# Hybrid decoder layer, 1 core: all tiles' normed rows turned from their buffers, operand sums from turned blocks, weight rows sooner, w_down sums in GpSimd's queue

## The chip, the core and the metric

The kernel runs on one core of a Trainium2 chip. The metric is the device time of one execution in microseconds, as a median over runs. The engines are TensorE (PE, matmuls and transposes), VectorE (DVE), ScalarE (ACT), GpSimd (POOL) and SyncE (SP). SP computes nothing here and issues most of the transfers; ACT and POOL issue a few. Each engine works through its own instructions in a fixed order.

## What is computed

One decoder layer on 2048 rows of width 1024, all in float32: a mixing part (window attention on one half of the width, a convolution group on the other), its output projection with a norm and the residual, and a gated feed-forward layer with a norm and the residual. The change touches the second half of it:

```python
hn = rms_norm(h, mix_pre_g)
proj = hn @ w_in
...
mixed = jnp.concatenate([attn_out, conv_out], axis=-1) @ w_out
h = h + rms_norm(mixed, mix_post_g)
hn = rms_norm(h, ffn_pre_g)
ff = (jax.nn.silu(hn @ w_gate) * (hn @ w_up)) @ w_down
h = h + rms_norm(ff, ffn_post_g)
```

## The kernel before

**Tiling.** The 2048 rows are four tiles `w` of 512 (`T`), each 4 × 128. A tile of an activation is held turned, 128 channels on the partitions and 512 rows along them; eight such blocks `k` (`KC`) make the width of 1024. A float32 product is made of three matmuls: each operand is split into a high part (a cast on ACT) and the rest, `lo` (a subtraction on DVE). One *product* here is four blocks `k` of three 128×512 matmuls, 12 in all.

**The feed-forward layer** runs in two passes, pass 0 over tiles 0 and 1, pass 2 over tiles 2 and 3. Each pass multiplies 2 × 2 blocks with seven products in place of eight: sums and differences of blocks (names `B11`, `B21`, `B22`, `T1` to `T4`) are multiplied and combined. Tile 0 or 2 supplies `B11` and `B21`, made by `stage_h_plain`; `stage_h_sums` makes `T1` to `T4` and `B22` from both tiles of a pass, for `k` = 0 to 3 in turn, with the tile `own` (0 or 2) and the other one.

**Phases on PE, in order:** the input projections (A), attention (B) and convolution (C), the output projection of each tile with its norm (W), then per pass `stage_pre` (40 products in pass 0, 32 in pass 2, on `B11` and then `B21`, labelled F; its partial results are stored in `keeps` and `mids`), `stage_p1` (labelled F, 22 rounds of 5 products in pass 0; it reads `keeps` and makes sums of weights on DVE) and `stage_p2` (labelled G, the second matrix). The prediction calls the `stage_p1` of pass 0 P1.0. A product whose accumulation goes on from a stored partial result starts with ACT writing that block into the PSUM bank: a *seed* (`mm@F<-gb@F`, L954 and L1066), loaded by SP from `keeps` into a buffer of the tag `gb`.

**Beside the main phase**, side jobs run in lanes: convolution taps (`fc@C`, on DVE), norms of later tiles, `stage_h_plain`, `stage_h_sums`, the end of a pass (`finish`), and `stage_tsums`, which makes the sums of `w_down` blocks (four blocks in, four sums out to `td`, eleven sets, for pass 0's G phase). Each job is a generator; its rate says how much of it is issued for each product. A scheduler then orders each engine's instructions and picks the buffers before the run. Tags have few buffers: `chl` 5, `at` 2, `gb` 2, `fc` 3, `wx` 1.

**Normed rows to turned blocks.** `norm_w` leaves the four normed row blocks of a tile in `xs` (four `chl` buffers). For tile 0 they stay there, and `stage_h_plain` turns them with `turn_row`: four PE transposes into one bank (`ct`), ACT copies it scaled into `gb`, ACT's queue stores it to `hT`. Tile 2 is turned in the norm. For tiles 1 and 3 ACT's queue stores the rows to `hn_scr` (L797); `stage_h_sums` later loads columns of them (`load_cols`, L820), and `turned` transposes these on PE (L842).

**Rounds of P1** (`stage_p1`): in step `nst - 2` a round fetches the next round's partial results, in the last step it loads the weight rows of the round after that.

Of the kernel before, what the change touches and what calls it, by code (L numbers as in the profile page):

```python
# [12 lines left out]
F32 = mybir.dt.float32  # L13
# [5 lines left out]
ALU = mybir.AluOpType  # L19
# [3 lines left out]
S = 2048  # L23
# [14 lines left out]
def layer_kernel(ctx, tc, x, xT, cols, rows, sinks, relb, onehot, w_in, w_pw, w_out, w_gate, w_up, w_down, out):  # L38
# [721 lines left out]
    def norm_w(w, acc):  # L760
        L = f"W{w}"
        lab[0] = L

        def whole(src):
            t = f4("chl")
            nc.sync.dma_start(t, src)
            return t

        gb = whole(rows[0].partition_broadcast(P))
        ssq = sm(4)  # L770
        for s in range(4):
            act(junk, acc[s], AF.Square, accum_out=ssq[:, s : s + 1])
            yield 0.75
            lab[0] = L
        r = rsqrt(ssq, 4, D, w < 3)
        xs = [whole(x[w * T + s * P : w * T + (s + 1) * P]) for s in range(4)]
        ssq2 = sm(4)
        yield 3
        for s in range(4):
            lab[0] = L  # L780
            stt(acc[s], acc[s], r[:, s : s + 1], gb, ALU.mult, ALU.mult)
            yield 1.25
            lab[0] = L
            vtt(acc[s], xs[s], acc[s], ALU.add)
            r0 = w * T + s * P
            nc.sync.dma_start(h_scr[r0 : r0 + P], acc[s])
            act(junk, acc[s], AF.Square, accum_out=ssq2[:, s : s + 1])
            yield 1.25
        lab[0] = L
        r2 = rsqrt(ssq2, 4, D, w < 3)  # L790
        yield 3
        for s in range(4):
            lab[0] = L
            act(xs[s], acc[s], AF.Copy, scale=r2[:, s : s + 1])
            if w % 2:
                r0 = w * T + s * P
                nc.scalar.dma_start(hn_scr[r0 : r0 + P], xs[s])  # L797
# [20 lines left out]
    def load_cols(w, k, tag):  # L818
        t = f2(tag, (P, 4, P))
        nc.sync.dma_start(t, hn_scr[w * T : (w + 1) * T, k * P : (k + 1) * P].rearrange("(s p) c -> p s c", p=P))  # L820
        return t

    def split_f(x, w):
        act(w[:, 0], x, AF.Copy)  # L824
# [13 lines left out]
    def turned(w, k, bank_of, tag):  # L838
        c = load_cols(w, k, tag)
        b = bank_of()  # L840
        for s in range(4):
            nc.tensor.transpose(b[:, s * P : (s + 1) * P], c[:, s], ident)  # L842
        return b
# [12 lines left out]
    def stage_h_plain(ws, ops, n, off):  # L856
        L = f"H{ws[0]}"
        for k in range(4):
            lab[0] = L
            if ws[0]:  # L860
                u = f2(COLTAG[ws[0]][k])
                nc.sync.dma_start(u, hT[ws[0] // 2][k + off])
            else:
                u = turn_row(0, normed, k + off)
                lab[0] = L
            o = op_tile(ws, ops, n, k, {})
            act(o[:, 0], u, AF.Copy)
            lo(u, o, False)
            yield 2.0

    def stage_h_sums(ws, ops):
        L = f"H{ws[0]}"
        spare = {}
        for k in range(4):
            lab[0] = L
            ct_ = COLTAG[ws[0]]
            g1, g2 = g_ffn[:, k : k + 1], g_ffn[:, k + 4 : k + 5]
# [11 lines left out]
            lab[0] = L  # L889
# [6 lines left out]
            for n, x in (("T1", r[:, 0]), ("T2", t[:, 0]), ("T3", r[:, 1]), ("T4", t[:, 1])):  # L896
# [95 lines left out]
    def stage_p1(ws, ops, mid, keep):  # L992
# [54 lines left out]
        for q, (m, j, i, nst) in enumerate(todo):  # L1047
# [60 lines left out]
            if j == nst - 1:  # L1108
                loads(m + 2)
            yield 2.76  # L1110

    def stage_tsums(td):
        L = "G0"
        for pr in range(NF // 2):
# [1 line left out]
            wx = f4("wx", (P, 2, T))  # L1116
            b = [wx[:, 0], wx[:, 1], f2("fc"), f2("fc")]
            for i, (f, n) in enumerate(((0, 0), (0, 1), (1, 0), (1, 1))):
                nc.sync.dma_start(b[i], w_down[2 * pr + f, :, n * T : (n + 1) * T])
            yield 3  # L1120
            b11, b12, b21, b22 = b
            for to, o, p_, q_ in ((0, b11, b12, b11), (2, b12, b22, b12), (1, b22, b22, b11), (3, b21, b21, b22)):
                lab[0] = L
                vtt(o, p_, q_, ALU.subtract)
                nc.sync.dma_start(td[to, pr], o)
# [412 lines left out]
```

## Time and profile before

| | us |
|---|---|
| median of 3 runs (lowest, highest) | 1996.32 (1993.41, 1996.72) |
| profiled execution | 1994.08 |
| its span | 1992.1 |
| PE busy in the span | 1936.4 |
| DVE busy | 1467.2 |
| ACT busy | 953.5 |
| POOL busy | 247.2 |

The profile is of one execution. Times in it count from the start of the span. A row of the view by stretches gives a window's start and end, its length, then for each engine the busy time and, in brackets, the instructions; PEclk is the share of TensorE's full clock that was granted, the DMA share the mean busy share of the core's 16 DMA engines. A row of the view of groups gives line, engine, operation, result <- operands, the count, then busy time and the mean of one in ns, then idle time ahead of it and what ended it. A row of the timeline gives start and duration, and in brackets the idle time before and its releaser. A row of transfers ends with the size of one and the median time from issue to landing. A name such as `gb@F` is the tag of a buffer and the phase that filled it.

### The profile page before, as it was taken

Reading aid. Unit: us, or ns where it says so; the run is one execution under the profiler, and the core shown is the slowest. Engines: PE = TensorE matmul, PEld = TensorE weight load, DVE = VectorE, ACT = ScalarE, POOL = GpSimd, SP = SyncE. Lnnn points to the kernel's source line nnn. Section 1 sums busy time; section 2 is a strip of 40 time slices with the busy share of each in tenths; the row PEclk is TensorE's granted clock in tenths of the full one; section 3 lists DMA queues with packets and bytes.
Section 4 is the critical chain, followed back from the end, with each engine's and each line's share of the span. In section 5 each row is a group of like instructions: output and inputs, shape, how many; then the busy total and the mean of one; then the engine's idle time right before and its main releaser. Section 6 shows DMA issues by size and latency. Waiting matters only on the chain.

```text
span 1992.1 us, 26622 instructions
## 1 busy us (share of the span) xinstructions
PE 1936.4 (97%) x8730; PEld 1550.4 (78%) x8730; DVE 1467.2 (74%) x2648; ACT 953.5 (48%) x1878; POOL 247.2 (12%) x339
## 2 busy tenths in 40 slices
PE   8999999999998999899999999998899999999997
PEld 6877777777776878678888788886788888888886
DVE  4999969995875899777659964667766765455557
ACT  5455354447546533234355464656543433345443
POOL 4011111101121000000000110000023332311003
PEclk9999999999999999999999999999999999999999
DMA  8786657566659767865478787759845542466664
GB/s 307 252 305 218 210 187 257 182 214 216 225 199 322 258 222 254 280 231 190 143 238 273 255 270 243 253 201 376 289 147 170 169 159 85 142 227 197 211 195 143
DMA packets 224810, 444.06 MB, mean 223 GB/s; under 512 B 22136, under 2 KB 47904, under 8 KB 224672
## 3 DMA queue, kind: packets, MB, share of 16 engines
q1 hardware_dynamic: 212768, 429.79, 64.8%
q10 hardware_dynamic: 11904, 12.59, 1.8%
q8 instruction: 68, 1.11, 0.2%
q14 instruction: 70, 0.57, 0.1%
HBM read 327.46 MB, written 114.83 MB: 222 GB/s over the span
## 4 chain that ended last, share of the span: by engine, by line
PE 77%; DMA 11%; DVE 6%; issue 2%; ACT 2%; POOL 1%; SPq 1%; DVEq 0%; POOLq 0%; ACTq 0%
PE mm@F L85 29%; PE mm@G L85 18%; PE mm@A L85 14%; PE mm@W L85 5%; PE tr@B L85 4%; PE tr@W L85 3%; DMA gb@F<-keeps 1%; DMA chl@F<-w_gate 1%; DMA raw@F<-w_gate 1%; PE mm@U L85 1%; DMA chl@G<-h_scr 1%; DVE fc@C L94 1%; DVE w@F L94 1%; DMA td<-fc@G 1%; PE tr@B L492 1%
## 5 line engine op out<-in xcount | busy, mean ns | idle before, releaser
L94 DVE SCALAR_TENSOR_TENSOR fc@C<-glu@C,colt,fc@C 128x512 f32<-128x512 f32 x480 | 357.1, 758 | 2.8
L85 PE MATMUL mm@F<-hl@H,w@F 128*128 128x512 f32 x1056 | 256.8, 394 | 8.1 <-ACT mm@F L954 8.1
L85 PEld LDWEIGHTS mm@F<-hl@H,w@F 128*128 128x128 f32 x1056 | 200.4, 190 | 51.5 <-ACT mm@F L954 9.5
L85 PE MATMUL mm@G<-hl@G,hl@G 128*128 128x512 f32 x924 | 228.0, 392 | 1.8 <-DVE hl@G L94 1.6
L85 PE MATMUL mm@A<-hl@A,w@A 128*128 128x512 f32 x840 | 209.4, 397 | 4.4 <-ACT w@A L127 1.8
L85 PEld LDWEIGHTS mm@G<-hl@G,hl@G 128*128 128x128 f32 x924 | 171.7, 188 | 38.9 <-DVE hl@G L94 2.4
L824 ACT ACTIVATE w@F<-chl@F 128x512 fp32r<-128x512 f32 x220 | 134.8, 624 | 138.9 <-PE mm@F L85 131.4
L85 PE MATMUL mm@G<-w@G,hl@G 128*128 128x512 f32 x876 | 199.4, 389 | 0.0
L85 PEld LDWEIGHTS mm@G<-w@G,hl@G 128*128 128x128 f32 x876 | 164.4, 188 | 34.1
L85 PEld LDWEIGHTS mm@A<-hl@A,w@A 128*128 128x128 f32 x840 | 156.6, 189 | 43.1 <-issue 3.1
L94 DVE TENSOR_TENSOR w@F<-chl@F,w@F 128x512 fp32r<-128x512 f32 x198 | 145.6, 739 | 37.9 <-ACT w@F L824 37.3
L85 PE MATMUL mm@F<-mid@H,w@F 128*128 128x512 f32 x528 | 137.4, 408 | 12.5 <-ACT mm@F L954 10.6
L85 PE MATMUL mm@F<-ql@H,w@F 128*128 128x512 f32 x528 | 128.5, 391 | 6.8 <-ACT mm@F L1066 4.8
L85 PE MATMUL mm@F<-p@H,w@F 128*128 128x512 f32 x528 | 132.5, 397 | 0.0
L85 PEld LDWEIGHTS mm@F<-mid@H,w@F 128*128 128x128 f32 x528 | 103.7, 198 | 36.8 <-ACT mm@F L954 11.9
L85 PE MATMUL mm@F<-x@H,w@F 128*128 128x512 f32 x528 | 126.7, 391 | 0.0
L85 PEld LDWEIGHTS mm@F<-ql@H,w@F 128*128 128x128 f32 x528 | 98.9, 188 | 29.3 <-ACT mm@F L1066 6.2
L85 PEld LDWEIGHTS mm@F<-p@H,w@F 128*128 128x128 f32 x528 | 101.7, 193 | 21.8 <-ACT at@F L1080 0.2
L85 PEld LDWEIGHTS mm@F<-x@H,w@F 128*128 128x128 f32 x528 | 98.4, 188 | 21.1 <-issue 0.8
L127 ACT ACTIVATE w@A<-raw@A 128x512 fp32r<-128x512 f32 x110 | 67.5, 626 | 92.3 <-PE mm@A L85 63.5
L94 DVE TENSOR_TENSOR w@G<-raw@G,w@G 128x512 fp32r<-128x512 f32 x73 | 52.1, 714 | 68.8 <-ACT w@G L824 67.7
L495 POOL TENSOR_SCALAR_AFFINE_SELECT p@B<-p@B 128x512 f32<-128x512 f32 x62 | 52.9, 863 | 361.2 <-ACT p@B L493 359.8
(302 smaller groups left out, 3224.8 us busy)
## 6 DMA issues: line engine op xcount, KB each, us to landing
mids<-fa@F SPq DMA_DIRECT2D x154, 256.0 KB, 2.6
raw@A<-w_in SPq DMA_DIRECT2D x55, 512.0 KB, 4.5
w@A<-lo_in SPq DMA_DIRECT2D x84, 256.0 KB, 3.5
fc@G<-mids SPq DMA_DIRECT2D x77, 256.0 KB, 3.5
fa@G<-mids SPq DMA_DIRECT2D x75, 256.0 KB, 4.2
gb@F<-keeps SPq DMA_DIRECT2D x72, 256.0 KB, 4.5
w@W<-fold SPq DMA_DIRECT2D x32, 512.0 KB, 5.3
chl@F<-w_gate SPq DMA_DIRECT2D x22, 512.0 KB, 4.0
```

The source lines that it names most:

```text
L85: r = nc.tensor.matmul(*args, **kw)
L94: r = op(*args, **kw)
L127: act(w[:, 0], raw, AF.Copy)
L492: nc.tensor.transpose(o[:, i * P : (i + 1) * P], pr[:, 4 * g + i], ident)
L495: nc.gpsimd.affine_select(out=pg[:, kb].rearrange("p (i q) -> p i q", q=P), in_=pg[:, 1].rearrange("p (i q) -> p i q", q=P), compare_op=AL ...
L824: act(w[:, 0], x, AF.Copy)
```

## The change

1. The rows of tiles 1, 2 and 3 are all turned at the end of `norm_w`, straight from `xs`, into `at` buffers. SP stores each turned block to `hT`, one turn after it was made. `hn_scr`, `load_cols` and `turned` are gone.
2. `stage_h_sums` loads two turned blocks of both tiles and forms the sums from these: four DVE operations for four, and five splits, per `k`; one cast of ACT less.
3. `stage_tsums` issues its 88 transfers from GpSimd's queue in place of SP's, and its yields and rate (`RT`) change.
4. `stage_p1` fetches partial results two steps sooner and loads weight rows two steps sooner; `y5` is in `at`, not in `gb`.
5. The sums of pass 2 (`S2`) may start after 8 steps of P2 in place of 16, but only when the job `E0.3` is done; rates of a few jobs change.

```diff
 act(xs[s], acc[s], AF.Copy, scale=r2[:, s : s + 1])
-if w % 2:
-    r0 = w * T + s * P
-    nc.scalar.dma_start(hn_scr[r0 : r0 + P], xs[s])
...
 if w == 0:
     normed.extend(xs)
-if w == 2:
-    for k in range(KC):
-        turn_row(w, xs, k)
-        yield 2.0
+    return
+late = []
+for k in range(KC):
+    late.append(turn_row(w, xs, k, "at"))
+    if k:
+        nc.sync.dma_start(hT[w // 2][w % 2, k - 1], late[k - 1])
+    yield 2.0
+nc.sync.dma_start(hT[w // 2][w % 2, KC - 1], late[-1])
...
-def turn_row(w, xs, k):
+def turn_row(w, xs, k, tag):
...
-    u = f2("gb")
+    u = f2(tag)
     act(u, b, AF.Copy, scale=g_ffn[:, k : k + 1])
-    nc.scalar.dma_start(hT[w // 2][k], u)
     return u
...
 # stage_h_sums, for k in range(4)
-own = t_("chl", (P, 2, T))
-nc.sync.dma_start(own, hT[ws[0] // 2][k :: 4].rearrange("j p t -> p j t"))
-own = own[:, 0], own[:, 1]
-b12 = turned(ws[1], k, tr, ct_[2])
-b22 = turned(ws[1], k + 4, tr, ct_[3])
+own, other = (t_("chl", (P, 2, T)) for _ in range(2))
+for j, b in enumerate((own, other)):
+    nc.sync.dma_start(b, hT[ws[0] // 2][j, k::4].rearrange("j p t -> p j t"))
+yield 2.5
+b = op_tile(ws, ops, "B22", k, spare)
+act(b[:, 0], other[:, 1], AF.Copy)
 r = t_("chl", (P, 2, T))
-t = t_("chl", (P, 2, T))
-act(r[:, 1], b12, AF.Copy, scale=g1)
-b = op_tile(ws, ops, "B22", k, spare)
-act(b[:, 0], b22, AF.Copy, scale=g2)
-yield 1.5
-stt(r[:, 0], b12, g1, own[0], ALU.mult, ALU.subtract)
-stt(t[:, 0], b22, g2, r[:, 0], ALU.mult, ALU.subtract)
-stt(r[:, 1], b22, g2, r[:, 1], ALU.mult, ALU.subtract)
-stt(b[:, 1], b22, g2, b[:, 0].bitcast(F32), ALU.mult, ALU.subtract)
-vtt(t[:, 1], own[1], t[:, 0], ALU.subtract)
-yield 3
+vtt(r[:, 0], other[:, 0], own[:, 0], ALU.subtract)
+vtt(r[:, 1], other[:, 1], r[:, 0], ALU.subtract)
+vtt(other[:, 0], other[:, 1], other[:, 0], ALU.subtract)
+lo(other[:, 1], b, False)
+vtt(own[:, 1], own[:, 1], r[:, 1], ALU.subtract)
+yield 2
...
 # stage_p1
-        y5 = f2("gb")
+        y5 = f2("at")
...
 if j == nst - 4:
+    fetch(m + 1)
     sums(m + 1)
-if j == nst - 2:
-    fetch(m + 1)
-if j == nst - 1:
+if j == nst - 3:
     loads(m + 2)
...
 # stage_tsums
-        nc.sync.dma_start(b[i], w_down[2 * pr + f, :, n * T : (n + 1) * T])
-    yield 3
+        nc.gpsimd.dma_start(b[i], w_down[2 * pr + f, :, n * T : (n + 1) * T])
+    yield 2.5
...
-        nc.sync.dma_start(td[to, pr], o)
-        yield 1
+        nc.gpsimd.dma_start(td[to, pr], o)
+        yield 0.6
...
-RT = 0.3
+RT = 0.2
...
-PRE_S0, PRE_S2 = 22, 16
+PRE_S0, PRE_S2 = 22, 8
...
-lh.rates = {"N1": 1.2, "S0": 0.9, "H0": 1.2}
-lf.rates = {n: 0.6 for n in ("O0.1", "O0.3", "E0.1", "E0.3")} | {n: 1.2 for n in ("Y0", "Y1", "O2.1", "O2.3")}
+lh.rates = {"N1": 1.2, "S0": 0.9, "B21.2": 1.2, "S2": 0.7}
+lf.rates = {n: 1.2 for n in ("O0.1", "O0.3", "E0.1", "E0.3")} | {n: 1.2 for n in ("Y0", "Y1", "O2.1", "O2.3")}
...
-lh.add("S2", stage_h_sums(ws, ops), lambda: f"P2.{PRE_S2}" in started)
+lh.add("S2", stage_h_sums(ws, ops), lambda: f"P2.{PRE_S2}" in started and "E0.3" in lf.done)
```

**PE in pass 0's `stage_pre`.** Each row is line, operation, result <- operands, shape, and a count where the next ones are alike; the numbers in a name tell one buffer's use from another. Before, the first transposes of loaded columns (`tr@H`) stand together after the 25th of the 40 products:

```order
L85 MATMUL mm@F_1010_6114<-hl@H_813_4982,w@F_992_6038 128x512 x3
L85 MATMUL mm@F_1010_6114<-hl@H_821_5029,w@F_992_6038 128x512 x3
L842 MATMUL tr@H_1002_6087<-ident,fc@H_1001_6085 128x128 x4
L842 MATMUL tr@H_1004_6094<-ident,at@H_1003_6092 128x128 x4
L842 MATMUL tr@H_1025_6191<-ident,fc@H_1024_6189 128x128 x4
L842 MATMUL tr@H_1027_6198<-ident,at@H_1026_6196 128x128 x4
L85 MATMUL mm@F_1015_6141<-hl@H_802_4928,w@F_995_6059 128x512 x3
L85 MATMUL mm@F_1015_6141<-hl@H_810_4971,w@F_995_6059 128x512 x3
```

In the changed kernel the transposes read the row buffers of the norm (`chl@W`) and write the bank `ct`. The last of the eight turns stands here, inside the 35th product (`mm@F_1085`):

```order
L85 MATMUL mm@F_1085_6455<-hl@H_802_4927,w@F_1071_6393 128x512 x3
L814 MATMUL ct@H_996_6040<-ident,chl@W_938_5731 128x128
L814 MATMUL ct@H_996_6040<-ident,chl@W_939_5733 128x128
L814 MATMUL ct@H_996_6040<-ident,chl@W_940_5735 128x128
L814 MATMUL ct@H_996_6040<-ident,chl@W_941_5737 128x128
L85 MATMUL mm@F_1085_6455<-hl@H_810_4970,w@F_1071_6393 128x512 x3
L85 MATMUL mm@F_1085_6455<-hl@H_813_4981,w@F_1071_6393 128x512 x3
```

The eight groups moved from before the middle of the stage's second half, some of them together, to one group in every two products up to its last fifth.

**DVE at the end of pass 0's `stage_pre`.** Before, the sums (`chl@H`) and splits of operands (`mid@H`, `p@H`, `hl@H`, `mb@H`) stand among the splits of weights (`w@F`):

```order
L94 TENSOR_TENSOR p@H_1065_6370<-chl@H_1052_6309,p@H_1065_6370 128x512
L94 SCALAR_TENSOR_TENSOR chl@H_1075_6413<-tr@H_1072_6401,colt,chl@H_1070_6397 128x512
L94 TENSOR_TENSOR w@F_1078_6423<-raw@F_1059_6343,w@F_1078_6423 128x512
L94 TENSOR_TENSOR mid@H_1066_6373<-chl@H_1053_6310,mid@H_1066_6373 128x512
L94 SCALAR_TENSOR_TENSOR chl@H_1076_6414<-tr@H_1074_6408,colt,chl@H_1075_6413 128x512
L94 SCALAR_TENSOR_TENSOR chl@H_1075_6413<-tr@H_1074_6408,colt,chl@H_1075_6413 128x512
L94 SCALAR_TENSOR_TENSOR hl@H_1077_6416<-tr@H_1074_6408,colt,hl@H_1077_6416 128x512
L94 TENSOR_TENSOR w@F_1083_6447<-raw@F_1079_6426,w@F_1083_6447 128x512
L94 TENSOR_TENSOR mb@H_1086_6468<-chl@H_1075_6413,mb@H_1086_6468 128x512
```

Now the last split of a weight of the stage (`w@F_1100`) comes first and the first operation of `stage_h_sums` stands right behind it:

```order
L94 TENSOR_TENSOR fa@F_1080_6440<-fa@F_1080_6440,mm@F_1079_6426 128x512
L94 TENSOR_TENSOR w@F_1100_6533<-raw@F_1090_6483,w@F_1100_6533 128x512
L94 TENSOR_TENSOR chl@H_1022_6169<-chl@H_1017_6143,chl@H_1016_6142 128x512
L94 TENSOR_TENSOR chl@H_1022_6169<-chl@H_1017_6143,chl@H_1022_6169 128x512
L94 TENSOR_TENSOR chl@H_1017_6143<-chl@H_1017_6143 128x512
L94 TENSOR_TENSOR hl@H_1021_6167<-chl@H_1017_6143,hl@H_1021_6167 128x512
L94 TENSOR_TENSOR chl@H_1016_6142<-chl@H_1016_6142,chl@H_1022_6169 128x512
L94 TENSOR_TENSOR mid@H_1023_6175<-chl@H_1022_6169,mid@H_1023_6175 128x512
L94 TENSOR_TENSOR fa@F_1093_6502<-fa@F_1093_6502,mm@F_1092_6488 128x512
L94 TENSOR_SCALAR fc@C_1099_6530<-glu@C_1098_6528,colt 128x512
```

From the first `chl@H_1022` row to the split of the first weight of P1.0, this piece's second last row, stand 57 instructions, with convolution taps (`fc@C`), `w_down` sums (`fc@G`, `wx@G`) and results of `stage_pre` (`fa@F`) among 35 of the 36 of `stage_h_sums`:

```order
L94 TENSOR_TENSOR ql@H_1087_6474<-chl@H_1082_6444,ql@H_1087_6474 128x512
L94 TENSOR_TENSOR chl@F_1110_6613<-chl@F_1110_6613,raw@F_1108_6609 128x512
L94 TENSOR_TENSOR p@H_1088_6477<-chl@H_1075_6415,p@H_1088_6477 128x512
L94 TENSOR_TENSOR fc@G_1126_6672<-fc@G_1126_6672,fc@G_1127_6673 128x512
L94 TENSOR_TENSOR w@F_1112_6619<-chl@F_1110_6613,w@F_1112_6619 128x512
L94 TENSOR_TENSOR chl@F_1111_6616<-raw@F_1108_6609,chl@F_1109_6611 128x512
```

All 36 stood before the stage's last weight split and now stand behind it.

**The queues of SP and POOL in P1.0.** Before, SP issues the `w_down` loads and `td` stores between weight rows (`chl@F`) and seeds (`gb@F`):

```order
L1125 DMA td<-fc@G_1372_8309 128x512
L1119 DMA wx@G_1403_8516<-w_down 128x512 x2
L1119 DMA fc@G_1404_8517<-w_down 128x512
L1008 DMA chl@F_1355_8184<-w_gate 128x1024
L1119 DMA fc@G_1405_8518<-w_down 128x512
L1094 DMA mids_4716<-fa@F_1310_7903 128x512
L1038 DMA gb@F_1351_8163<-keeps_4719 128x512
L1125 DMA td<-wx@G_1403_8516 128x512 x2
```

The same set of blocks (`wx@G_1403` there, `wx@G_1405` here) stands on POOL with no other work around it:

```order
L1102 DMA fc@G_1377_8333<-w_down 128x512
L1108 DMA td<-wx@G_1375_8331 128x512
L1108 DMA td<-fc@G_1377_8333 128x512
L1102 DMA wx@G_1405_8523<-w_down 128x512 x2
L1108 DMA td<-fc@G_1376_8332 128x512
L1102 DMA fc@G_1406_8524<-w_down 128x512
L1102 DMA fc@G_1407_8525<-w_down 128x512
L1108 DMA td<-wx@G_1405_8523 128x512 x2
```

**PE in pass 2's `stage_pre`.** The last turns of tile 3 stand among the first blocks (`mid@H_2045`) of four products; the next matmul needs the second block, `mid@H_2047`:

```order
L85 MATMUL mm@F_2142_12802<-mid@H_2045_12331,w@F_2129_12740 128x512 x3
L814 MATMUL ct@H_1976_11904<-ident,chl@W_1921_11605 128x128
L814 MATMUL ct@H_1976_11904<-ident,chl@W_1922_11607 128x128
L814 MATMUL ct@H_1976_11904<-ident,chl@W_1923_11609 128x128
L814 MATMUL ct@H_1976_11904<-ident,chl@W_1924_11611 128x128
L814 MATMUL ct@H_1978_11918<-ident,chl@W_1921_11605 128x128
L814 MATMUL ct@H_1978_11918<-ident,chl@W_1922_11607 128x128
L814 MATMUL ct@H_1978_11918<-ident,chl@W_1923_11609 128x128
L814 MATMUL ct@H_1978_11918<-ident,chl@W_1924_11611 128x128
L85 MATMUL mm@F_2123_12713<-mid@H_2047_12336,w@F_2109_12651 128x512
```

Before, transposes of loaded columns stood in this stage one or two groups at a time; now these last four groups have three matmuls between the first three and none between the last two.

More of the change, by code (lines that the diff above doesn't have):

```diff
@@ L241, in layer_kernel @@
     glu_scr = dr.tile([4, P, S], F32, name="glu_scr")
-    hn_scr = dr.tile([S, D], F32, name="hn_scr")
     y_scr = dr.tile([4, P, S], F32, name="y_scr")
-    hT = [dr.tile([KC, P, T], F32, name=f"hT{i}") for i in range(2)]
+    hT = [dr.tile([2, KC, P, T], F32, name=f"hT{i}") for i in range(2)]
     qs = {}
@@ L800, in norm_w @@
             normed.extend(xs)
-        if w == 2:
-            for k in range(KC):
-                turn_row(w, xs, k)
-                yield 2.0
+            return
[3 more added lines that the diff above has]
+            if k:
+                lab[0] = f"H{w}"
+                nc.sync.dma_start(hT[w // 2][w % 2, k - 1], late[k - 1])
+            yield 2.0
+        lab[0] = f"H{w}"
+        nc.sync.dma_start(hT[w // 2][w % 2, KC - 1], late[-1])
     normed = []
-    def turn_row(w, xs, k):
+    def turn_row(w, xs, k, tag):
         lab[0] = f"H{w}"
@@ L836, in layer_kernel @@
     COLTAG = {0: ["fc", "at", "fc", "at"], 2: ["fc", "at", "fc", "at"]}
[L838 to L843, printed above, removed]
     def op_tile(ws, ops, n, k, spare):
@@ L861, in stage_h_plain @@
                 u = f2(COLTAG[ws[0]][k])
-                nc.sync.dma_start(u, hT[ws[0] // 2][k + off])
+                nc.sync.dma_start(u, hT[ws[0] // 2][0, k + off])
             else:
-                u = turn_row(0, normed, k + off)
+                u = turn_row(0, normed, k + off, "gb")
                 lab[0] = L
+                nc.scalar.dma_start(hT[0][0, k + off], u)
             o = op_tile(ws, ops, n, k, {})
@@ L875, in stage_h_sums @@
             lab[0] = L
-            ct_ = COLTAG[ws[0]]
-            g1, g2 = g_ffn[:, k : k + 1], g_ffn[:, k + 4 : k + 5]
-            own = t_("chl", (P, 2, T))
-            nc.sync.dma_start(own, hT[ws[0] // 2][k :: 4].rearrange("j p t -> p j t"))
-            own = own[:, 0], own[:, 1]
-            b12 = turned(ws[1], k, tr, ct_[2])
-            b22 = turned(ws[1], k + 4, tr, ct_[3])
-            r = t_("chl", (P, 2, T))
-            t = t_("chl", (P, 2, T))
-            act(r[:, 1], b12, AF.Copy, scale=g1)
-            b = op_tile(ws, ops, "B22", k, spare)
-            act(b[:, 0], b22, AF.Copy, scale=g2)
-            yield 1.5
-            lab[0] = L
-            stt(r[:, 0], b12, g1, own[0], ALU.mult, ALU.subtract)
-            stt(t[:, 0], b22, g2, r[:, 0], ALU.mult, ALU.subtract)
-            stt(r[:, 1], b22, g2, r[:, 1], ALU.mult, ALU.subtract)
-            stt(b[:, 1], b22, g2, b[:, 0].bitcast(F32), ALU.mult, ALU.subtract)
-            vtt(t[:, 1], own[1], t[:, 0], ALU.subtract)
-            yield 3
-            for n, x in (("T1", r[:, 0]), ("T2", t[:, 0]), ("T3", r[:, 1]), ("T4", t[:, 1])):
+            own, other = (t_("chl", (P, 2, T)) for _ in range(2))
+            for j, b in enumerate((own, other)):
+                nc.sync.dma_start(b, hT[ws[0] // 2][j, k::4].rearrange("j p t -> p j t"))
+            yield 2.5
+            lab[0] = L
+            b = op_tile(ws, ops, "B22", k, spare)
+            act(b[:, 0], other[:, 1], AF.Copy)
+            r = t_("chl", (P, 2, T))
+            vtt(r[:, 0], other[:, 0], own[:, 0], ALU.subtract)
[4 more added lines that the diff above has]
+            yield 2
+            for n, x in (("T1", r[:, 0]), ("T2", r[:, 1]), ("T3", other[:, 0]), ("T4", own[:, 1])):
                 lab[0] = L
```

4 lines of the change are left out of this document (removed).

## The prediction

> **What bounds the kernel now.** I read the page first, then busy time by stretches for the stages the change touches, then who waited for whom inside them. TensorE (PE) is busy 97% of the span, so a change matters where it adds or removes PE idling; the question is where the idle time lies.
>
> ```profile
> span 1992.1 us, 26622 instructions
> PE 1936.4 (97%) x8730; PEld 1550.4 (78%) x8730; DVE 1467.2 (74%) x2648; ACT 953.5 (48%) x1878; POOL 247.2 (12%) x339
> ...
> 1003.64 2.20 PE L85 MATMUL mm@F<-ql@H,w@F 128*128 128x512 f32 x9
> 1005.68 4.70 PE L85 MATMUL mm@F<-hl@H,w@F 128*128 128x512 f32 x20
> ...
> core 0: us, PE busy (x) PEld busy (x) DVE busy (x) ACT busy (x) POOL busy (x), PEclk, DMA share, GB/s
> 610.71:682.21 71.50, 62.62 (x273) 50.48 (x272) 50.78 (x81) 46.26 (x82) 0.00 (x0) 0.95 0.89 301
> 1327.33:1438.02 110.69, 98.22 (x418) 79.31 (x416) 88.11 (x187) 74.76 (x145) 0.52 (x1) 0.94 0.96 338
> ...
> 682.21:780.00 97.79, 95.60 (x412) 77.94 (x411) 88.28 (x144) 35.72 (x64) 0.00 (x0) 0.98 0.68 225
> 780.00:900.00 120.00, 108.52 (x447) 87.11 (x446) 94.81 (x153) 39.38 (x71) 0.00 (x0) 0.94 0.78 263
> 900.00:1013.80 113.80, 113.80 (x505) 94.26 (x504) 80.68 (x126) 46.98 (x83) 0.00 (x0) 1.00 0.52 168
> ```
>
> Nine matmuls from 1003.64 to 1005.68 are 0.227 us each without a stall, so a product of 12 is 2.72 us. With that pace each stage's loss follows, idle time and slow clock together. The last 20 products of pass 0's `stage_pre` begin at 610.71; 240 matmuls are 54.4 us and the 32 transposes 4.9 (below), so of 71.5 us 12.2 are lost. The first FFN phase of pass 0 (P1.0, 682.21 to 1013.8, 331.6 us) holds 1364 PE records, 309.2 us: 22.4 lost, all before 900, for from there PE is busy throughout. Pass 2's `stage_pre` (384 matmuls, 87.1, and 4.9) loses 18.7 of 110.7. These 53 us are what the change can win or spend.
>
> **What causes the losses.** In pass 0 the normed rows of tile 1 leave in one burst on ACT's queue, and a weight load comes late behind it:
>
> ```profile
> 609.48 0.34 ACTq L797 DMA_DIRECT2D hn_scr<-chl@W  x1
> ...
> hn_scr<-chl@W ACTq DMA_DIRECT2D x4, 512.0 KB, 8.5
> ...
> 622.39 0.63 ACT L824 ACTIVATE w@F<-raw@F 128x512 fp32r<-128x512 f32 x1 [3.52 <-DMA raw@F<-w_gate]
> ...
> 624.05 1.22 PE L85 MATMUL mm@F<-hl@H,w@F 128*128 128x512 f32 x2 [3.71 <-ACT mm@F L954]
> ```
>
> The seed that PE waited for stands behind the weight cast on ACT. In P1.0 the late one is another seed, behind the `w_down` loads and `td` stores in SP's queue:
>
> ```profile
> 863.49 1.93 SPq L1119 DMA_DIRECT2D wx@G<-w_down  x2
> 865.51 0.38 SPq L1119 DMA_DIRECT2D fc@G<-w_down  x1
> ...
> 867.37 0.42 SPq L1038 DMA_DIRECT2D gb@F<-keeps  x1
> ...
> 874.13 0.60 ACT L1066 ACTIVATE mm@F<-gb@F 128x512 f32<-128x512 f32 x1 [6.59 <-DMA gb@F<-keeps]
> ...
> SPq L1125 <- DVE wx@G L94: 21.2, 15, 4.3
> SPq L1119 <- DMA td<-fc@G: 21.0, 9, 4.7
> SPq L1119 <- DMA td<-wx@G: 15.8, 8, 4.2
> ...
> SPq L1125 <- DVE fc@G L94: 10.7, 17, 1.6
> ...
> PE mm@F L85 <- DVE gb@F L94: 5.0, 3, 2.2
> PE mm@F L85 <- ACT mm@F L1066: 4.8, 2, 4.5
> ```
>
> SP stood 68.7 us in these four waits, with seeds and weight rows queued behind.
>
> **The change, part by part: pass 0's turns.** Instruction counts on PE and DVE do not change; their places do. Eight turns of four transposes stand two products apart, the last three matmuls into the 35th of 40 products. The old transposes price them, their busy time being a little over what they occupy:
>
> ```profile
> L842 PE MATMUL tr@H<-ident,at@H 128*128 128x128 f32 x16 | 2.5, 276 | 0.7 <-DVE chl@H L94 0.7
> L842 PE MATMUL tr@H<-ident,fc@H 128*128 128x128 f32 x16 | 2.4, 272 | 0.0
> ...
> chl@H<-hT SPq DMA_DIRECT2D x3, 512.0 KB, 4.8
> ...
> 700.00:750.00 50.00, 48.78 (x206) 39.84 (x207) 46.54 (x76) 18.62 (x34) 0.00 (x0) 0.97 0.66 216
> ...
> 610.71 1.52 PE L85 MATMUL mm@F<-hl@H,w@F 128*128 128x512 f32 x6
> ...
> 682.21 1.52 PE L85 MATMUL mm@F<-ql@H,w@F 128*128 128x512 f32 x6
> ```
>
> From 610.71, 14 products (38.1), three matmuls (0.7) and 32 transposes (4.9) put the last turn's end at 654.4, with 1 us for a stall that stays at 655.4. Until then the four rows hold four of the five `chl` buffers, and the first `other` block of `stage_h_sums` can be loaded only after: 4.8 us. What VectorE (DVE) then has before P1.0's first product is the point. Before, the sums stood among the weight splits; now all stand behind the last split, mixed with conv taps and `w_down` sums, 57 instructions in order to the split of P1.0's first weight. A DVE that rarely waits does 76 in 46.54 us, 0.612 each: 34.9 us, and 1 us for waits on ACT's casts. P1.0 starts at 655.4 + 4.8 + 34.9 + 1 = 696.1 instead of 682.21: **+13.9**, the relief of the burst already counted. PE has ended its own products near 671 and idles some 25 us. Bounds: no stall in the stage and DVE at its pace alone, +10; the 12.2 us lost as before with 4 us more for load and casts, +24.
>
> **The clock.** Stretches with long stalls show a lower granted clock:
>
> ```profile
> 1360.00:1420.00 60.00, 47.53 (x194) 37.35 (x193) 47.48 (x98) 37.18 (x70) 0.00 (x0) 0.89 1.01 350
> ```
>
> 47.53 busy us at 0.89 are 5.2 us lost to the clock around several stalls; an idle of 25 us costs part of it, **+2** (0 to 4).
>
> **P1.0.** SP loses 88 issues and the four waits, to GpSimd's queue, where nothing else stands (POOL x0 above). Seeds and rows are asked for two products sooner, 5.4 us; the worst seed was 6.59 late. Counting DVE instructions to each weight split against PE's products, the splits run 3 to 16 us ahead after some ten products; at the start the second weight's split comes about 2 us after PE wants it. I keep 9 of the 22.4 lost: 2 there, 7 for seeds still late and `w_down` blocks that DVE waits for. **−13.4**; bounds −22.4 and +4 (queue slower, as in the rival). DVE keeps its 88.28 of 97.79 us, so it has no reserve for such waits early on. This trace has no transfer in GpSimd's queue. By the nearest rows a block lands in about 4 us and so does a store:
>
> ```profile
> wx@G<-w_down SPq DMA_DIRECT2D x20, 256.0 KB, 4.0
> td<-fc@G SPq DMA_DIRECT2D x22, 256.0 KB, 3.5
> ```
>
> Ten sets of four blocks pass between 682 and 900, 22 us each; a set takes at least 4.0 + four sums (2.4) + 3.5 = 10 us, since the one `wx` buffer is not free sooner. The spare 12 us hide a slower queue, and I cost it at nothing. The Trainium skill, "SBUF — State Buffer", section "SBUF: two separate sides", warns against this very move: while DVE runs a two-port instruction GpSimd cannot write descriptors, and it gives 620 ns growing to 3100 ns beside a copy. By its "Who interferes with whom" a two-input `tensor_tensor` has no such mode, and the groups of DVE here are nearly all of that kind, so by the skill the sum stays; no run here yet shows it.
>
> **Pass 2.** Four turns of tile 3 stand apart, then four in one clump in the 17th round of products, three matmuls between, because `at` has two buffers and each is freed by a store. The second block of B21 needs one of them.
>
> ```profile
> PE mm@F L85 <- ACT mm@F L954: 10.6, 4, 4.1
> ...
> raw@F<-w_gate SPq DMA_DIRECT2D x12, 256.0 KB, 6.1
> ...
> at@H<-hn_scr SPq DMA_DIRECT2D x4, 256.0 KB, 6.8
> ...
> 1327.33 2.88 PE L85 MATMUL mm@F<-ql@H,w@F 128*128 128x512 f32 x12
> ...
> 1438.02 2.20 PE L85 MATMUL mm@F<-hl@H,w@F 128*128 128x512 f32 x9
> ```
>
> The clump ends near 1327.3 + 16 × 2.72 + 4.9 + 1.4 = 1377. A store and then a load in this crowded stretch take some 6 us each, cast and split 1.3: PE idles to 1391, about 14 us, 2 more at the fourth block, 2 for the clock, 2 for loads as late as now: 20 against 18.7 lost, **+1**. Bounds −8 (a store that went before lets the load start at once) and +7. `y5` in `at` and the spread of the `w_down` sums (the same work in 270 as in 257 units of the plan) lie under PE time: nothing; without cover, a store's 4 us at a handful of products.
>
> **The sum.** 13.9 + 2 − 13.4 + 1 = +3.5. The profiled execution took 1994.1 us (its span and 2.0 around it), 2.2 under the median 1996.3; so 1997.6 there, **2000** beside the median.
>
> **Rivals.** *A, the queue relief wins* (chance 0.30). P1.0 gives back 21 of 22.4, since both delays that PE shows there go away, and pass 2's store is early: 11 + 1 − 21 − 5 = −14, 1982. For it: PE stands still after 900 in no place, where the sets are done. Against: DVE starts P1.0 without a lead.
>
> *B, GpSimd's queue is slow* (0.17). If each load and store takes more than 6 us longer, the spare 12 us of a set are gone and DVE, which works in order, waits for `w_down` blocks with weight splits behind. Four us for each of some six sets fill P1.0's losses to where they were: 16 + 24 − 22.4 + 1 = +18, 2014. Against it: POOL has nothing else to do. The Trainium skill, "DMA: Bandwidth & Descriptors", section "Specifications", gives 1 us to the first byte on GpSimd's path against 0.6: 0.8 us a set, far from the point.
>
> *C, the burst was not the cause* (0.10). The same bytes now go as 256 KB stores with an `at` buffer waited for by ACT, in a stretch at 301 GB/s; the 12.2 us lost stay, the last turn comes 10 us later and P1.0 with it: 2010. For it: transfers there are 0.89 of the time busy already; against: single stores, 5.4 us apart.
>
> **How the numbers follow.** My forecast, that a later start of P1.0 is just not paid for by its smoother run, has 0.43. A measurement of this kernel tells about 0.2% (4 us) from nothing. The forecast's own spread is 1990 to 2008; it stands 0.18 slower, 0.15 same, 0.10 faster; A is faster but for 0.03 same, B and C slower. So faster 0.37, same 0.18, slower 0.45. The range reaches from A's upper part, 1984, to B, 2016.
>
> **What would show it.** The first matmul of P1.0 after 690 with PE idle over 15 us ahead and DVE busy throughout confirms the first term; a start before 685 refutes it. PE busy over 210 us between the start of P1.0 and 218 us later confirms the third; waits of DVE for `w_down` of over 10 us speak for B; waits of ACT's weight casts in `stage_pre` for C. In pass 2 the longest PE idle should follow the clump of turns. I am wrong if P1.0 starts on time, or if the loss there returns from another wait.

## The result and the profile after

| | before | changed |
|---|---|---|
| median, us | 1995.47 (4 runs, 1993.41 to 1996.72) | 2009.43 (4 runs, 2007.17 to 2010.97) |
| profiled execution, its span | 1994.08, 1992.1 | 2010.72, 2009.0 |

The ratio is 1.0065, with a 95% interval of 1.0052 to 1.0078: the change makes the kernel 14 us slower. The profiled executions differ by 16.6 us. The first lines of the page of the changed kernel:

```profile
span 2009.0 us, 26707 instructions
PE 1929.7 (96%) x8730; PEld 1545.5 (77%) x8730; DVE 1467.7 (73%) x2648; ACT 962.6 (48%) x1886; POOL 294.4 (15%) x427
```

PE and DVE have as many instructions as before. DVE is as busy (1467.2 before) and PE 6.7 us less (1936.4 before), in a span that is 16.9 us longer. So the time is idle PE: 79.3 us of the span where it was 55.7. The timeline of PE has the largest piece right where P1.0 starts (start, duration, in brackets the idle time before and its releaser):

```profile
655.44 0.60 PE L814 MATMUL ct@H<-ident,chl@W 128*128 128x128 f32 x4
655.79 15.94 PE L85 MATMUL mm@F<-hl@H,w@F 128*128 128x512 f32 x69
695.24 1.22 PE L85 MATMUL mm@F<-mid@H,w@F 128*128 128x512 f32 x2 [23.51 <-ACT w@F L820]
698.25 1.22 PE L85 MATMUL mm@F<-ql@H,w@F 128*128 128x512 f32 x2 [1.79 <-ACT w@F L820]
```

The last turn ended at 655.8, `stage_pre` at 671.7, and PE stood 23.5 us for P1.0's first weight. The row names ACT's cast; DVE's timeline says what that cast and its split stood behind:

```profile
655.62 0.69 DVE L94 TENSOR_TENSOR w@F<-raw@F,w@F 128x512 fp32r<-128x512 f32 x1
661.69 0.69 DVE L94 TENSOR_TENSOR chl@H<-chl@H,chl@H 128x512 f32<-128x512 f32 x1 [5.37 <-DMA chl@H<-hT]
...
693.84 0.69 DVE L94 TENSOR_TENSOR chl@F<-chl@F 128x512 f32<-128x512 f32 x1
...
698.65 0.69 DVE L94 TENSOR_TENSOR w@F<-chl@F,w@F 128x512 fp32r<-128x512 f32 x1
```

DVE waited for the first turned blocks until 661.7, then worked with 2.6 us of waits until P1.0 had its weights. The weight sum at 693.84 was cast on ACT and let PE start at 695.24; the first split followed at 698.65. By stretches (columns as before the change), the end of pass 0's `stage_pre`, P1.0 and pass 2's `stage_pre` of the changed kernel:

```profile
611.37:695.24 83.87, 58.94 (x274) 48.08 (x272) 46.83 (x75) 47.22 (x82) 5.38 (x10) 0.89 0.84 278
695.24:1022.46 327.22, 317.48 (x1361) 258.91 (x1362) 265.33 (x425) 126.28 (x222) 39.83 (x74) 0.98 0.65 216
1337.20:1455.20 118.00, 96.67 (x417) 77.43 (x416) 87.24 (x187) 77.66 (x150) 1.29 (x1) 0.90 0.92 324
```

Against 71.5, 331.9 and 110.7 before: +12.4, −4.7, +7.3. With 0.7 us of a later start and some 1.5 between P1.0 and pass 2 this is the 17 us of the spans. In pass 2 PE's timeline shows two waits:

```profile
1388.53 0.66 PE L814 MATMUL ct@H<-ident,chl@W 128*128 128x128 f32 x4 [0.47 <-ACT at@H L816]
1394.49 1.12 PE L814 MATMUL ct@H<-ident,chl@W 128*128 128x128 f32 x4 [5.31 <-ACT at@H L816]
1406.77 1.65 PE L85 MATMUL mm@F<-mid@H,w@F 128*128 128x512 f32 x3 [11.17 <-ACT mid@H L857]
```

A turn waits for ACT to empty the bank of the one before, and ACT for a store to free an `at` buffer; then the second B21 block waits for its load into `at`. ACT's own timeline for the turns, and the transfers of this stretch with their time to landing:

```profile
1393.75 0.69 ACT L816 ACTIVATE at@H<-ct@H,colt 128x512 f32<-128x512 f32 x1 [5.28 <-DMA hT<-at@H]
1397.55 0.69 ACT L816 ACTIVATE at@H<-ct@H,colt 128x512 f32<-128x512 f32 x1 [3.11 <-DMA hT<-at@H]
...
hT<-at@H SPq DMA_DIRECT2D x5, 256.0 KB, 5.9
at@H<-hT SPq DMA_DIRECT2D x2, 256.0 KB, 7.1
```

### The profile page after: what moved, and what is told of

Same layout as the page of the kernel before. It is cut to its first block, busy times and chain, and to the rows that moved or that the text cites. A ratio compares the mean times of both kernels' runs of the same rounds, so it can differ in the third digit from the quotient of the medians.

```text
span 2009.0 us, 26707 instructions
## 1 busy us (share of the span) xinstructions
PE 1929.7 (96%) x8730; PEld 1545.5 (77%) x8730; DVE 1467.7 (73%) x2648; ACT 962.6 (48%) x1886; POOL 294.4 (15%) x427
## 4 chain that ended last, share of the span: by engine, by line
PE 77%; DMA 10%; DVE 7%; issue 3%; POOL 2%; ACT 1%; SPq 0%; DVEq 0%; POOLq 0%; ACTq 0%
PE mm@F L85 33%; PE mm@G L85 16%; PE mm@A L85 13%; PE mm@W L85 5%; PE tr@B L85 4%; PE tr@W L85 2%; DVE fc@C L94 2%; DMA fc@G<-w_down 1%; PE mm@U L85 1%; DMA chl@H<-hT 1%; DMA td<-wx@G 1%; DVE hl@G L94 1%; PE tr@B L491 1%; PE ct@H L814 1%; DMA hT<-at@H 1%
## 5 line engine op out<-in xcount | busy, mean ns | idle before, releaser
L85 PE MATMUL mm@F<-mid@H,w@F 128*128 128x512 f32 x528 | 136.2, 405 | 42.8 <-ACT w@F L820 23.5
L85 PEld LDWEIGHTS mm@F<-p@H,w@F 128*128 128x128 f32 x528 | 99.1, 188 | 21.3 <-ACT at@F L1064 0.8
```

What stands on the lines that cost most here:

```text
L85: r = nc.tensor.matmul(*args, **kw)
```

## The experiments

Each experiment ran beside the kernel before on the same chip; the medians of the kernel before lay between 1995.5 and 1997.2 us. "P1.0" is the time from its first matmul to the first of the next phase, and "pass 2" that of pass 2's `stage_pre`; both kernels stand first. The last three columns are from one profiled execution each. Executions of one kernel lie 4 to 12 us apart, so differences of a few us in these columns are a hint, not a measurement.

| run | ratio to before (95%) | median us | P1.0 starts | P1.0 us | pass 2 us |
|---|---|---|---|---|---|
| before | | 1995.5 | 682.2 | 331.9 | 110.7 |
| changed | 1.0065 (1.0052 to 1.0078) | 2009.4 | 695.2 | 327.2 | 118.0 |
| e_turn | 1.0066 (1.0047 to 1.0085) | 2009.9 | 693.5 | 327.9 | 116.3 |
| e_noturn | 0.9931 (0.9908 to 0.9954) | 1981.1 | 681.3 | 319.4 | 109.8 |
| e_fetch | 0.9960 (0.9946 to 0.9975) | 1988.1 | 681.6 | 326.7 | 111.4 |
| e_ts | 0.9977 (0.9965 to 0.9990) | 1992.1 | 684.8 | 323.7 | 111.8 |
| a_early | 1.0047 (1.0032 to 1.0062) | 2006.5 | 691.8 | 331.0 | 117.0 |
| a_early3 | 1.0215 (1.0198 to 1.0232) | 2040.7 | 691.4 | 327.3 | 94.3 |
| a_tsold | 1.0061 (1.0046 to 1.0076) | 2009.7 | 691.5 | 327.9 | 116.8 |
| n_swap | 0.9958 (0.9939 to 0.9976) | 1987.8 | 682.0 | 325.9 | 111.5 |
| a_swap | 1.0061 (1.0040 to 1.0082) | 2008.5 | 692.4 | 330.2 | 116.2 |
| a_b21mb | 1.0034 (1.0019 to 1.0049) | 2003.1 | 693.4 | 327.3 | 109.2 |
| a_nohold | 1.0105 (1.0079 to 1.0131) | 2018.5 | 708.5 | 323.9 | 120.2 |
| n_nohold | 0.9945 (0.9926 to 0.9964) | 1987.0 | 688.3 | 321.6 | 112.9 |

### The parts alone

**e_turn**: the changed kernel with the rounds of P1 (with the tag of `y5`) and the `w_down` sums (with `RT`) put back.

```diff
-if j == nst - 4:
-    fetch(m + 1)
-    sums(m + 1)
-if j == nst - 3:
-    loads(m + 2)
+if j == nst - 4:
+    sums(m + 1)
+if j == nst - 2:
+    fetch(m + 1)
+if j == nst - 1:
+    loads(m + 2)
...
-nc.gpsimd.dma_start(td[to, pr], o)
-yield 0.6
+nc.sync.dma_start(td[to, pr], o)
+yield 1
```

> The kernel before with the turns, the sums from turned blocks and the job rates alone; rounds of P1 and the w_down sums as before. Theory 1 (the late turns cost by themselves what the changed kernel's trace shows: 13 us until P1.0 starts, 7 us in pass 2, and P1.0's own 24 us stay lost): 2014 to 2019 us, P1.0 starting near 695. Theory 2 (the w_down sums in GpSimd's queue, which DVE waits for ahead of P1.0, are part of that 13): P1.0 starts near 691 or sooner, total under 2012.

Measured: 2009.9 us, P1.0 from 693.5. The turns alone cost what the whole change costs. The start lies between the two theories, nearer theory 1's 695, so the `w_down` sums take part in it with 2 us at most; the total is under 2012 for another reason, that P1.0 lost 4 us less than before (327.9).

**e_noturn**: the kernel before with these edits (and the rates of the O0 and E0 jobs) and without the turns.

```diff
+nc.gpsimd.dma_start(b[i], w_down[2 * pr + f, :, n * T : (n + 1) * T])
...
+if j == nst - 4:
+    fetch(m + 1)
+    sums(m + 1)
+if j == nst - 3:
+    loads(m + 2)
```

> The kernel before with sooner rounds of P1 and the w_down sums in GpSimd's queue with their new spread, without the turns. Theory 1 (the smoother P1.0 is real, and in the changed kernel only its DVE work that comes late eats it): P1.0 loses 10 us or less of the 24, total 1981 to 1986 us. Theory 2 (DVE waits for w_down blocks whatever the turns do): P1.0 loses 17 us or more, total 1988 to 1994.

Measured: 1981.1 us, ratio 0.9931 (0.9908 to 0.9954), the fastest of all kernels run here. P1.0 takes 12.5 us less than before; against 307.4 us for its 1356 matmuls at 0.2267 it loses 12, not quite theory 1's 10. So the relief that the prediction counted exists, and with the turns most of it is gone. Not all of it is shorter waits: PE's idle time in P1.0 fell from 13.7 to 8.2 us and its busy time from 318.2 to 311.2, at a granted clock of 1.00 where it was 0.97.

**e_fetch** and **e_ts** make one half of these edits each (and leave the rates of the jobs alone):

```diff
 # e_fetch alone
+    fetch(m + 1)
     sums(m + 1)
-if j == nst - 1:
+if j == nst - 3:
     loads(m + 2)
 # e_ts alone
-nc.sync.dma_start(td[to, pr], o)
+nc.gpsimd.dma_start(td[to, pr], o)
-RT = 0.3
+RT = 0.2
```

> The kernel before with only the sooner fetch and loads of P1 and y5 in at. Theory 1 (late seeds are what PE loses P1.0's time on, and asking 5.4 us sooner is enough): 1983 to 1988 us. Theory 2 (they are late because of what stands ahead in SP's queue, so asking sooner moves them little): 1991 to 1995.

> The kernel before with only the w_down sums in GpSimd's queue and their new spread. Theory 1 (the queue relief is worth half of P1.0's loss): 1982 to 1988 us. Theory 2 (the sets come closer together, 17 us for 20, and DVE waits for their blocks): 1993 to 2000.

Measured: 1988.1 and 1992.1 us. The first lies just above theory 1's range, the second just under theory 2's; their gains of 8 and 4 us add up to 12 of e_noturn's 15. In e_fetch PE waits for DVE's sums alone, as the view of waits of P1.0 shows (engine, line, waited for, us in total, times, longest). Its idle time there did not fall (14.3 us, 13.7 before); what it gained in P1.0 is PE's busy time, 312.4 us against 318.2. With both edits the waits are little over half:

```profile
PE mm@F L85 <- DVE at@F L94: 11.2, 6, 3.5
PE mm@F L85 <- DVE fa@F L94: 3.1, 2, 2.9
```

and of e_noturn:

```profile
PE mm@F L85 <- DVE fa@F L94: 3.9, 3, 2.0
PE mm@F L85 <- DVE at@F L94: 3.7, 5, 2.0
```

### Earlier turns

**a_early**: the turns close together, stored at once, with two tags.

```diff
-late.append(turn_row(w, xs, k, "at"))
-if k:
-    nc.sync.dma_start(hT[w // 2][w % 2, k - 1], late[k - 1])
-yield 2.0
+late.append(turn_row(w, xs, k, ("at", "gb")[k % 2]))
+nc.sync.dma_start(hT[w // 2][w % 2, k], late[k])
+yield 1.0
```

> The changed kernel with the turns of tiles 1 to 3 close together: one yield of 1.0 after each, stored at once, buffers from at and gb in turn. On PE tile 1's eight turns now end four matmuls into the stage's 22nd product in place of the 35th; tile 3's still end late in pass 2. Theory 1 (P1.0 starts late because the last turn is late and DVE then has the whole stage_h_sums before it; the same lateness keeps DVE full and lets the w_down waits reach PE): P1.0 starts at 680 to 685, P1.0 takes 317 to 321 us, total 1984 to 1990. Theory 2 (the relief of P1.0 is lost to something else that the turns bring, such as the buffers): P1.0 starts at 680 to 685 but takes 326 or more, total 1993 to 1998.

Measured: 2006.5 us; P1.0 starts at 691.8. The 331.0 us of P1.0 are theory 2's, the late start is neither's: the last turn now comes at 626 and no long wait stands ahead of P1.0, but the time went into the turns themselves: between 600 and 682.2 PE idles 14.4 us (8.9 before) at a granted clock of 0.90 (0.96). Two of eight on PE's timeline, and the stretch around them:

```profile
619.93 1.11 PE L811 MATMUL ct@H<-ident,chl@W 128*128 128x128 f32 x4 [0.78 <-ACT gb@H L813]
621.87 1.11 PE L811 MATMUL ct@H<-ident,chl@W 128*128 128x128 f32 x4 [0.83 <-ACT at@H L813]
...
606.00:640.00 34.00, 21.15 (x79) 14.90 (x78) 12.01 (x20) 19.65 (x30) 2.21 (x6) 0.75 0.79 240
```

With one bank a turn costs 1.9 us when turns follow each other, 0.8 of it waiting for ACT, and the clock granted over these 34 us is 0.75. Between products, a turn of the changed kernel takes 0.35 us of PE (655.44 to 655.79 above). Spacing them was right for PE; it is what makes the last one late.

**a_early3**: tile 3's turns use more buffers, and the order puts all eight ahead of pass 2's `stage_pre`.

```diff
-late.append(turn_row(w, xs, k, ("at", "gb")[k % 2]))
+late.append(turn_row(w, xs, k, ("at", "gb", "mb", "mb")[k % 4] if w == 3 else ("at", "gb")[k % 2]))
```

> As the run a_early, and tile 3's turns use the buffers at, gb, mb, mb in turn, by which all eight stand on PE before pass 2's stage_pre begins. Theory 1 (in pass 2 PE waits for the stores that free the two at buffers, then for B21's load): that stage falls from 118 us to 95 to 102, total 15 to 20 us under a_early. Theory 2 (that stretch is bound by transfers, whose share is near 1.0 of the time): it stays at 108 or more, as before, total 7 to 10 us under a_early.

Measured: 2040.7 us, 34 above a_early and outside both ranges. The stage fell to 94.3 us, its matmuls and hardly more, a little below theory 1's range: transfers do not bind it. But the same PE order now has turns waiting for the norm in the phase before (waits of PE between 1260 and 1392):

```profile
PE ct@H L811 <- ACT chl@W L793: 22.4, 4, 20.7
PE tr@W L85 <- ACT chl@W L719: 11.3, 1, 11.3
PE mm@G L85 <- ACT hl@G L817: 9.1, 3, 7.8
```

The order puts the turns where the normed rows are not ready: the first turn waited 20.7 us for them.

### Pass 2's buffers

**a_b21mb**: the second and fourth block of tile 2's B21 no longer share `at` with the turns.

```diff
-u = f2(COLTAG[ws[0]][k])
+u = f2("mb" if n == "B21" and k % 2 else COLTAG[ws[0]][k])
```

> The changed kernel with the second and fourth block of tile 2's B21 loaded into mb in place of at, so that they wait for no store of tile 3's turns. Theory 1 (in pass 2 PE stands still because the loads of B21 and the turns share two at buffers): the stage's two long stalls (5.3 and 11.2 us) go, the stage falls from 118 to 100 to 108 us, total 1996 to 2002. Theory 2 (the later last turn, 293 instead of 233 PE instructions into the stage, then delays stage_h_sums as in pass 0): the stalls move to the start of the next phase, the stage stays at 112 to 120, total 2004 to 2011.

Measured: 2003.1 us, the stage 109.2 against 118.0: both a little over theory 1's ranges, and below theory 2's. PE's view of waits between 1330 and 1460 now has one entry, a seed's:

```profile
PE mm@F L85 <- ACT mm@F L938: 12.1, 4, 6.3
```

This shows the shared buffers as the cause of the two stalls of 5.3 and 11.2 us. What is left is the wait for seeds, 12.1 us; the kernel before has 10.6 of it there, the changed kernel 3.9.

### What eats P1.0's relief

**a_tsold**: the changed kernel with the `w_down` sums as before.

```diff
-nc.gpsimd.dma_start(td[to, pr], o)
-yield 0.6
+nc.sync.dma_start(td[to, pr], o)
+yield 1
...
-RT = 0.2
+RT = 0.3
```

> The changed kernel with the w_down sums as before: SP's queue, old yields and rate. Theory 1 (with the late turns P1.0's relief is eaten by DVE's waits for w_down blocks, whichever queue carries them): 2006 to 2012 us, P1.0 at 325 to 329 us. Theory 2 (the closer sets in GpSimd's queue are what eats it): P1.0 at 322 or less, total under 2005. Theory 3 (GpSimd's queue helps also here): P1.0 at 331 or more, total over 2013.

Measured: 2009.7 us, P1.0 327.9, as theory 1 has it: with the turns GpSimd's queue is not seen to help or harm. This leaves open whether DVE's waits for the blocks are the reason.

**n_swap** and **a_swap**: the order of a set's loads, on e_noturn and on the changed kernel.

```diff
-for i, (f, n) in enumerate(((0, 0), (0, 1), (1, 0), (1, 1))):
+for i, f, n in ((0, 0, 0), (1, 0, 1), (3, 1, 1), (2, 1, 0)):
```

> The run e_noturn with the loads of a w_down set in another order: the block that DVE's second sum needs (b22) is loaded ahead of b21 and takes the fc buffer that comes free first. Theory 1 (DVE waits for w_down blocks because the second of two fc buffers comes free only when a td store has landed, and these waits reach PE): DVE's waits for w_down fall from 9.5 us to 5 or less, total 1975 to 1979. Theory 2 (DVE's waits do not reach PE there): total 1979 to 1983.

> The changed kernel with that same order of the w_down loads. Theory 1 (the 17.6 us of waits for w_down, against 9.5 without the turns, are why P1.0 takes 327 us and not 319): waits 11 or less, P1.0 at 319 to 323 us, total 2001 to 2006. Theory 2 (P1.0 is long because DVE has less done when it starts): P1.0 at 325 to 329, total 2007 to 2011.

Measured: 1987.8 and 2008.5 us. Both are misses for theory 1, and n_swap lies above theory 2's range too. In a_swap DVE's waits for `w_down` fell from 17.6 to 11.2 us and P1.0 was not shorter (330.2); in n_swap they were 10.8 (9.5 in e_noturn), and the total is 7 us above e_noturn's, though the intervals of the two ratios overlap. So nothing shows that waits for `w_down` make P1.0 long.

**a_nohold** and **n_nohold**: taps may run before `stage_h_sums` is done.

```diff
-lc.hold = lambda: "S0" not in lh.done
```

> The changed kernel without the line that holds the convolution taps back until stage_h_sums is done. On DVE taps then fill the time before the last turn, and 47 instructions instead of 57 stand between the first sum and P1.0's first weight; the last turn itself stands 34 PE instructions (8 us) later. Theory 1 (P1.0 takes 327 us and not 319 because DVE idles before the last turn, and what it did not do then fills it in P1.0): P1.0 starts at 694 to 700 and takes 316 to 321 us, total 2000 to 2006. Theory 2 (P1.0's length hangs on the order of single loads and seeds, not on how much DVE has left): P1.0 at 325 or more, total 2008 to 2014.

> The run e_noturn without that line. Theory 1: DVE has done more when P1.0 starts, P1.0 at 313 to 319 us, total 1973 to 1980. Theory 2: P1.0 at 320 to 328 us as in the other orders tried, total 1981 to 1992.

Measured: 2018.5 and 1987.0 us. DVE did 106 instructions in place of 75 before P1.0 in a_nohold, and P1.0 fell only to 323.9, between the two theories; its start fell back to 708.5, later than expected, with PE waiting 32.0 us, and the total is outside both ranges; n_nohold is theory 2's. So the DVE work left at the start goes with 3 of the 8 us between the changed kernel and e_noturn. The line is worth keeping in the changed kernel; without the turns the intervals of the two ratios overlap.

The view by stretches answers more than these runs did. The first 20 us of P1.0 in the changed kernel and a later stretch with a stall, then the first 20 us and the whole of P1.0 in e_noturn:

```profile
695.24:715.24 20.00, 18.21 (x64) 13.92 (x65) 18.85 (x32) 8.86 (x15) 5.91 (x11) 0.78 0.74 243
...
875.24:895.24 20.00, 17.60 (x69) 13.73 (x68) 15.93 (x27) 7.64 (x15) 4.31 (x8) 0.91 0.80 274
```

```profile
681.29:701.29 20.00, 20.00 (x90) 16.57 (x89) 19.96 (x33) 8.81 (x16) 7.09 (x14) 1.00 0.81 277
...
681.29:1000.66 319.37, 311.16 (x1363) 254.27 (x1361) 261.84 (x420) 123.15 (x216) 44.70 (x83) 1.00 0.67 225
```

After its long wait PE does 64 matmuls in 20 us at a clock of 0.78, in e_noturn 90 at 1.00: 26 × 0.227 = 5.9 us, 1.8 of it the wait for the second weight and 4.1 the clock. Over the whole of P1.0 the changed kernel's PE is busy 317.5 us for 1361 matmuls, e_noturn's 311.2 for 1363. That is 6.3 of the 7.8 us between them: slower matmuls, not more waiting. And e_turn, with nearly the same pause ahead (22.0 us), loses the same at the start. Its first 20 us, its whole P1.0 and that of the kernel before:

```profile
693.46:713.46 20.00, 18.21 (x65) 14.31 (x66) 18.89 (x31) 8.70 (x15) 0.00 (x0) 0.79 0.78 260
...
693.46:1021.32 327.86, 317.50 (x1361) 259.53 (x1362) 265.79 (x425) 125.57 (x223) 0.00 (x0) 0.97 0.66 218
...
682.21:1014.07 331.86, 318.19 (x1363) 259.50 (x1362) 263.77 (x421) 122.08 (x218) 0.00 (x0) 0.97 0.66 219
```

Against 307.4 us, and without 5.4 to 5.9 us for this restart, e_turn loses 15 in P1.0 and the changed kernel 14, the kernel before 24.5, e_noturn 12. So with the late start, and the restart left out, most of the relief is there without the two edits. Length less busy time gives PE's idle time in P1.0: 13.7 us before, 10.4 in e_turn, 9.7 in the changed kernel, 8.2 in e_noturn. With the turns the waits are shorter with or without the two edits, and the busy time stays near 318 us. This is consistent with loads and seeds getting ahead while PE stands, which no run has separated from the order. The pause is not the whole of it: a_early has the two edits and no pause ahead of P1.0, and PE is busy 314.1 us there but idles 16.9. Why the relief is missing there stays open.

## Why the prediction was right, and where it was not

The forecast was 2000 us and slower, the measured time 2009.4 is inside 1984 to 2016. The sum was +3.5 us and the change cost 14: the direction rests on the first term; P1.0 gave back less than was put, and pass 2 cost more.

**The start of P1.0 (+13.9) held.** Last turn's end 655.4 forecast and 655.8 measured, first sum on DVE 660.2 and 661.7, P1.0 696.1 and 695.2, idle PE 25 and 23.5 us. The path, from the last turn over the load and the counted DVE instructions to the first weight, is what the trace shows. That the figures came out within 1.5 us is partly luck. Eight turns took 2.8 us of PE (0.35 each) where 4.9 was put, and waits and slow matmuls made up for it. The split to which the prediction counted ended at 699.3, not at 696.1; PE needed only the cast for its first matmul and began 4 us before. The start is not under 685, which was the refutation. Of rival C little is seen: one wait of 1.4 us, at 616, is all that PE has from 605 to the end of the stage.

**P1.0 (−13.4, of which 2 for the clock is taken back) was the step that failed in size.** The clock and P1.0 together were −11.4; −4.7 was measured. Against the 309.2 us that the prediction took for the matmuls, the changed kernel loses 18.0. The clock and the second weight cost 5.9 of it where 4 was put (2 each), and 12 us of further losses stayed where 7 was put. The sign named for this term, PE busy over 210 us in the first 218 us of P1.0, did not come: 208.3 (204.3 before). The term itself was about right for a kernel without the turns: −12.5 in e_noturn. What failed is adding the two terms up: e_turn has 327.9 us in P1.0 without any relief edit, the changed kernel 327.2 with them. That the late start and the relief act on the same losses fits these two runs; a_early (331.0 us without the pause) shows that the turns also take the relief in another way. Over half of the relief in e_noturn is faster matmuls (7.0 us less busy time); the changed kernel's matmuls got only 0.7 us faster, with the restart alone costing 4.

**Pass 2 (+1) was mis-sized at its upper bound, +7.** The load that waits for a store was priced (14 us for a store, a load and a split; 11.2 measured). That the turns themselves wait for the same two buffers was not: 5.3 us on the last turn, before the store and load begin. In all PE idles 21.3 us in the stage where 18 was put, and the clock (0.90) costs some 4.7 where 2 was put: 96.7 us busy against 87.1 for the matmuls and 4.9 for the transposes as priced.

**Rival B** (GpSimd's queue is slow) is refuted. Its transfers between 682 and 930 land in 4.0 to 4.8 us, those of SP's queue in the kernel before in 3.5 to 4.0 (682 to 900), and the rival needed over 6 us more for each:

```profile
fc@G<-w_down POOLq DMA_DIRECT2D x20, 256.0 KB, 4.8
td<-wx@G POOLq DMA_DIRECT2D x20, 256.0 KB, 4.0
td<-fc@G POOLq DMA_DIRECT2D x20, 256.0 KB, 4.2
...
wx@G<-w_down POOLq DMA_DIRECT2D x18, 256.0 KB, 4.1
```

The sign that the prediction named for B did appear: DVE waits 15.0 us in P1.0 for blocks of the sets (8.4 before). But it does not belong to the queue, for with the sets in SP's queue (a_tsold) these waits are 13.2 us and P1.0 is as long.

The warning of the Trainium skill, "SBUF — State Buffer", section "SBUF: two separate sides", thus does not decide here. By that page's "Who interferes with whom" two-input instructions leave GpSimd's writing alone, and the landing times beside a DVE that is 81% busy in P1.0 (265.33 of 327.22 us) agree.

**Rival A** (the relief wins) did not come true. Only e_noturn, which leaves out the turns, has a total near its 1982 (1981.1), and that is a coincidence: P1.0 gave back 12.5 us there and not 21, and the rival's late start is missing.

Open stays which single order makes P1.0 319 us in e_noturn and 322 to 326 in its two variants; each edit moves the whole order, and these variants differ by as much as the effects sought. Part of it can be the spread of executions: e_noturn's 319 us are from its fastest one (1978.8 us), the variants' from executions of 1989.0 and 1990.0.

## What to carry to other kernels

When work reads its input from scarce buffers instead of from memory, its last step is when those buffers come free. Count, in the engine's own order, what must follow that step before the next phase can begin. Two effects that may act on the same idle time need not add; run each part alone before keeping the sum. Here one half of the change alone gains 15 us (0.9931, 0.9908 to 0.9954), the other alone costs 14, and both together cost 14. The pause of TensorE was dearer than its length: behind the pauses of 23.5 and 22.0 us the slower clock cost some 4 us more.

## What the runs showed of the hardware

Not every stall costs clock. In e_noturn the granted clock stays 1.00 through P1.0 with 8.2 us of idle PE, in single stalls of 2.0 us at most. In the changed kernel, with 9.7 us, the 20 us stretches around the waits of 23.5 and 1.8 us, of 2.7 and of 1.9 us show 0.78, 0.91 and 0.91, but the stretch from 895.24 with another wait of 1.9 us shows 1.00. What makes the difference no run here shows. Around transposes that follow each other through one PSUM bank, each waiting 0.8 us for ACT, the granted clock over 34 us was 0.75 (a_early).
